# 64 instead of 32 tokens of the second layer gather the rows of their own experts, and 44 instead of 40 blocks of activations stay on chip

## The chip, the cores and the metric

The kernel runs on one core of a Trainium2 chip. The metric is device time in microseconds of one execution. Before the change it is 2793.98 us, the median of three runs (2786.86 to 2801.69). TensorE multiplies 128x128 matrices held as weights with up to 512 columns, VectorE and ScalarE work on tiles of 128 partitions, GpSimd (POOL) issues the gathers, SyncE (SP) and ScalarE issue the other transfers; all transfers run on the core's 16 DMA engines.

## The reference

Two layers over 512 tokens (256 of context, 256 latent, 1024 features). Each layer has four parallel mixers (neighbourhood attention, an mLSTM, latent attention, window attention) and then an expert stage, which is what matters here:

```python
def peer_ffn(h, wq, sub_keys, u, v):
    ...
        eidx = jnp.take_along_axis(cand_i, fpos, axis=-1)
        gate = jax.nn.softmax(fs, axis=-1)
        act = jax.nn.gelu(jnp.einsum('td,thkd->thk', xb, u[eidx]).astype(F32), approximate=False)
        w = (gate * act).astype(xb.dtype)
        return jnp.einsum('thk,thkd->td', w, v[eidx])
```

Each token chooses 128 of 16384 experts (8 heads, 16 each). For every chosen expert it takes the dot product with that expert's row of u (1024 floats), a gelu, a gate, and adds the row of v with that weight. In the second layer only the 256 latent tokens go through it.

## The kernel before, in words

Two ways of doing the expert stage stand side by side. Most tokens are done densely: all 16384 rows of u, as 128 blocks of 128 experts, are multiplied with all tokens (the U blocks), and all rows of v likewise (the V blocks); the gates are a matrix that is zero where a token did not choose an expert. A few tokens, the ones "apart", are done by gathering: GpSimd fetches the rows of u and v that these tokens chose, and VectorE makes the dot products and sums.

`APART` holds their number for each layer (128 and 32). With fewer than 128 such tokens each has 128/n partitions, each partition serving n of its 128 experts; in the second layer that is four partitions of 32 before. One gather (line 1409) fetches one row of 4 KB for each of 128 partitions, 0.524 MB; there are n of them for u, each followed by a multiplication with a sum on VectorE (line 1415, tile `junk`), and n for v, each followed by a multiply-add (lines 1420 and 1422, tile `facc`). At the end `facc` is added over a token's partitions with a matmul (line 1548, `fsel`). `wd` is the number of tokens left for the dense way: 224 in the second layer.

A U block: SP loads two blocks at once (line 1446, tile `raw`, two buffers of 1 MB), ScalarE rounds a block to the short format of TensorE (line 1448, tile `spl`, ten buffers), VectorE takes the remainder (line 1449), TensorE makes 24 matmuls with `wd` columns (three products, lines 72 to 74, for each of 8 slices), ScalarE the gelu (line 1466). The activations of the first 2 x `FOLD` blocks stay on chip (`kept`), the others are stored (`ad`) and loaded again for V.

Gates: for every 8 tokens VectorE builds three kinds of one-hot tiles (lines 1351, 1352, 1354), TensorE multiplies them (line 1368, 16 matmuls), ScalarE copies the part of the blocks that are not kept (line 1371, `gstage`), which is stored for every 32 tokens (line 1377, `gd`), and VectorE multiplies the kept activations in place (line 1375).

A V block: SP loads rows of v (line 1489), the gates of four blocks (line 1494, `vg`) and the activations of two (line 1497, `va`); VectorE multiplies gates and activations (line 1503, for blocks that were not kept), ScalarE and VectorE split weights (1504, 1505) and rows (1508, 1509) in two parts, and TensorE makes for each of 8 slices one matmul with both parts of the weights side by side (line 1519, 2 x `wd` columns) and one with `wd` columns (line 1521).

The program is written as loops of Python generators: `u_next` (line 1143 on) interleaves U blocks with gathers so that `PHASE1` steps of gathering are done by the last U block, and `rows_to` spreads the remaining ones over the first 58 pairs of V. In U, gathered rows take turns with the blocks in the ten `spl` buffers; in V they have four buffers of their own (`ROWS`). A scheduler that runs when the program is built then sets the order on each engine; the engines run that order without changing it. SP's transfers too are issued in that order, so one that has to wait holds up those behind it.

Of the kernel before, what the change touches and what calls it, by code (L numbers as in the profile page):

```python
# [29 lines left out]
PIECE = 3  # L30
F_ML, F_NA, F_MLA, F_SW = (1.3, 2.0), (1.0, 1.2), (1.2, 1.2), (1.2, 1.0)
RN, GW, GL = (2, 1), 1.4, (3, 3)
FOLD, QS, VA = (0, 20), (10, 6), (2, 3)

CTX = slice(0, TC)
LAT = slice(TC, TA)
APART = (128, 32)
ROWS = 4
PHASE1 = (144, 26)

C_ID = 0
C_RS = 128
# [11 lines left out]
class Kernel:  # L54
# [39 lines left out]
    def build(self):  # L94
        tc, nc, A = self.tc, self.nc, self.A
        with ExitStack() as es:
# [24 lines left out]
            self.ms = cst.tile([128, 4], F32, name="ms")  # L121
            self.wd = [TA - APART[0], TC - APART[1]]
            self.gd = [self.dram.tile([self.wd[l] // 32, 128, 128, 32], F32, name=f"gd{l}") for l in range(L)]
# [919 lines left out]
    def peer(self, l):  # L1043
# [4 lines left out]
        wd = self.wd[l]  # L1048
        apart = APART[l]
        t0 = apart // 128  # L1050
        with ExitStack() as es:
# [14 lines left out]
            def u_pair():  # L1066
                i = next(ublk, None)
                if i is not None:
                    used[0] += 1
                    self.u_blocks(l, i, dh, dl, wd)  # L1070
            with ExitStack() as e1:
# [45 lines left out]
                with ExitStack() as e2:  # L1117
# [20 lines left out]
                    def rows_to(n):  # L1138
                        while sp is not None and s0[0] < n:
                            s0[0] += 1  # L1140
                            next(sp, None)

                    def u_next():
                        u_pair()
                        rows_to(PHASE1[l] * (used[0] - u0) // (64 - u0))
                    for n, _ in enumerate(routes[t0]):
# [32 lines left out]
                with ExitStack() as e2:  # L1179
# [16 lines left out]
                    for n, i in enumerate(self.v_order(l)):  # L1196
                        rows_to(PHASE1[l] + (2 * apart - PHASE1[l]) * n // 58 if n < 58 else 300)
                        self.v_blocks(l, n, i, acc, ts, w - wd)
# [158 lines left out]
    def gates(self, l, t, g, hot):  # L1357
# [6 lines left out]
        for q in range(2):  # L1364
# [7 lines left out]
            if nf:  # L1372
                o = t * 128 + g * 8 + 4 * q - APART[l]
                f = self.kept[:, :, o:o + 4]
                nc.vector.scalar_tensor_tensor(f, pg[:, :nf], 1.0 / GSCALE, f, op0=ALU.mult, op1=ALU.mult)
        if g % 4 == 3:
            nc.scalar.dma_start(self.gd[l][4 * t + g // 4 - APART[l] // 32][:, nf:], self.gst)

# [439 lines left out]
```

## Time and profile before

| | before |
|---|---|
| median of the runs | 2793.98 us |
| the profiled execution, its own time | 2801.05 us |
| its span, first to last instruction | 2799.3 us |
| TensorE busy | 2628.3 us (94%) |
| VectorE busy | 2168.7 us (77%) |
| ScalarE busy | 1249.8 us (45%) |
| GpSimd busy | 490.9 us (18%) |
| DMA | 691.48 MB, mean 247 GB/s |

The shares are means over the whole program. The second layer's expert stage lies in the last 810 us of the span: its queries until about 2080, the U blocks until about 2425, the V blocks after that. A busy TensorE is not one at its peak, since matmuls overlap: how fast it goes is seen from the starts of successive matmuls. A DMA share can go over 1, since it adds up the durations of packets, which overlap.

### The profile page before, as it was taken

The page shows a single profiled execution, that of the slowest core. Times are in us where ns is not written, and L with a number is a line of the kernel's source. Part 1 is how long each engine was busy: PE and PEld are TensorE (multiplying, and loading weights), DVE is VectorE, ACT ScalarE, POOL GpSimd, SP SyncE. Part 2 cuts the span into 40 slices and gives each one's busy share as a digit, 9 for nine tenths or more (in the row PEclk, how much of TensorE's full clock was granted, in tenths as well). Part 3 has the DMA queues.
Part 4 walks back from the last instruction along what each step waited for, and adds up shares of the span by engine and source line. Part 5 has one row for each costly group of instructions (what it writes and reads, how often), then busy time and mean ns, then how long its engine had stood idle before and what let it go on. Part 6 is the DMA issues. An engine that isn't in the chain of part 4 may idle for free. (4 is left out here: it accounts for less than half of the span.)

```text
span 2799.3 us, 44568 instructions
## 1 busy us (share of the span) xinstructions
PE 2628.3 (94%) x17143; PEld 2407.9 (86%) x17143; DVE 2168.7 (77%) x4499; ACT 1249.8 (45%) x2059; POOL 490.9 (18%) x419
## 2 busy tenths in 40 slices
PE   8989899999999999799999998988999999998998
PEld 5766768999998898799999997767899999898987
DVE  5665757999998886699999886565788777677776
ACT  4564645334344433343333334554545444444443
POOL 0010000003443234233333320000001111111110
PEclk9999899999999999899999999999999999999999
DMA  7110424647998989989999993211535787998984
GB/s 264 69 61 31 166 89 157 220 159 246 347 359 337 340 321 378 338 322 386 382 367 384 372 364 125 76 39 68 201 137 191 270 283 282 333 319 294 333 306 167
DMA packets 275733, 691.48 MB, mean 247 GB/s; under 512 B 18016, under 2 KB 145376, under 8 KB 266048
## 3 DMA queue, kind: packets, MB, share of 16 engines
q1 hardware_dynamic: 196608, 448.12, 45.6%
q0 software_dynamic: 46080, 167.79, 15.9%
q10 hardware_dynamic: 32832, 72.72, 6.9%
q8 instruction: 134, 2.20, 0.3%
q14 instruction: 79, 0.65, 0.1%
HBM read 616.56 MB, written 71.57 MB: 246 GB/s over the span
## 5 line engine op out<-in xcount | busy, mean ns | idle before, releaser
L72 PE MATMUL pu<-h2h,spl 128*128 128x384 f32 (+1 forms) x2048 | 637.8, 311 | 37.1 <-ACT spl L1448 28.0
L74 PE MATMUL pu<-h2h,spl 128*128 128x384 f32 (+1 forms) x2048 | 629.6, 308 | 2.9 <-DVE spl L1449 2.9
L73 PE MATMUL pu<-h2l,spl 128*128 128x384 f32 (+1 forms) x2048 | 630.2, 308 | 0.0
L72 PEld LDWEIGHTS pu<-h2h,spl 128*128 128x128 f32 x2048 | 394.2, 192 | 44.9 <-ACT spl L1448 32.7
L74 PEld LDWEIGHTS pu<-h2h,spl 128*128 128x128 f32 x2048 | 393.5, 192 | 4.8 <-DVE spl L1449 4.6
L73 PEld LDWEIGHTS pu<-h2l,spl 128*128 128x128 f32 x2048 | 394.2, 192 | 0.3
L1509 DVE TENSOR_TENSOR spl<-raw,spl 128x1024 fp32r<-128x1024 f32 x256 | 305.7, 1220 | 98.2 <-ACT spl L1508 92.5
L1448 ACT CAST spl<-raw 128x1024 fp32r<-128x1024 f32 x256 | 266.3, 1051 | 249.2 <-DMA raw<-in_ut 92.3
L1508 ACT CAST spl<-raw 128x1024 fp32r<-128x1024 f32 x256 | 261.9, 1051 | 256.5 <-DMA raw<-in_v 173.6
L1449 DVE TENSOR_TENSOR spl<-raw,spl 128x1024 fp32r<-128x1024 f32 x256 | 311.7, 1224 | 44.1 <-ACT spl L1448 32.6
L73 PE MATMUL f<-wt,spl 128*128 128x384 f32 x1024 | 343.2, 335 | 0.0
L74 PE MATMUL f<-wt,spl 128*128 128x384 f32 x1024 | 336.3, 334 | 0.0
L72 PE MATMUL f<-wt,spl 128*128 128x384 f32 x1024 | 288.4, 337 | 2.1 <-ACT spl L1508 1.9
L1519 PE MATMUL f<-wt,spl 128*128 128x448 f32 x1024 | 251.1, 372 | 17.1 <-ACT spl L1508 11.7
L1409 POOL DMA_INDIRECT spl<-in_un,ix x97 | 131.6, 1357 | 704.8 <-DVE fp L1263 241.6
L1466 ACT ACTIVATE act<-pu 128x384 f32<-128x384 f32 (+1 forms) x216 | 93.7, 436 | 299.3 <-PE pu L74 268.8
L1519 PEld LDWEIGHTS f<-wt,spl 128*128 128x128 f32 x1024 | 186.0, 190 | 33.3 <-ACT spl L1508 15.0
L427 DVE TENSOR_TENSOR spl<-raw,spl 128x512 fp32r<-128x512 f32 (+1 forms) x226 | 149.8, 702 | 64.0 <-ACT spl L423 55.0
L73 PEld LDWEIGHTS f<-wt,spl 128*128 128x128 f32 x1024 | 193.0, 188 | 0.5 <-issue 0.5
L74 PEld LDWEIGHTS f<-wt,spl 128*128 128x128 f32 x1024 | 191.6, 188 | 0.0
L72 PEld LDWEIGHTS f<-wt,spl 128*128 128x128 f32 x1024 | 187.9, 189 | 3.2 <-ACT spl L1508 2.2
L1409 POOL DMA_INDIRECT row<-in_vn,ix x87 | 125.7, 1445 | 369.6 <-DVE facc L1422 313.0
(326 smaller groups left out, 5029.2 us busy)
## 6 DMA issues: line engine op xcount, KB each, us to landing
raw<-in_ut SPq DMA_DIRECT2D x128, 1024.0 KB
raw<-in_v SPq DMA_DIRECT2D x128, 1024.0 KB
ad<-act ACTq DMA_DIRECT2D x64, 384.0 KB
gd<-gstage ACTq DMA_DIRECT2D x12, 2048.0 KB
vg<-gd SPq DMA_DIRECT2D x32, 768.0 KB
va<-ad SPq DMA_DIRECT2D x64, 384.0 KB
raw<-in_win SPq DMA_DIRECT2D x22, 1024.0 KB
raw<-in_wq SPq DMA_DIRECT2D x16, 1024.0 KB
```

Of the source, the lines that this page charges most:

```text
L72: mm(ps, ah, bh, start=first, stop=False, **kw)
L73: mm(ps, ah, bl, start=False, stop=False, **kw)
L74: mm(ps, al, bh, start=False, stop=last, **kw)
L427: return eng.tensor_tensor(p[1][o], w[:, o], p[0][o].bitcast(F32), op=ALU.subtract)
L1409: nc.gpsimd.indirect_dma_start(r, None, tabs[which], bass.IndirectOffsetOnAxis(ix[:, s:s + 1], 0))
L1448: self.pin(nc.scalar.copy(uh, self.u[:, n % 2]), n < 3)
L1449: self.pin(nc.vector.tensor_tensor(ul, self.u[:, n % 2], uh.bitcast(F32), op=ALU.subtract), n < 3)
L1466: nc.scalar.activation(a[:, b, :w], ps[:, :w], AF.Gelu)
L1508: nc.scalar.copy(vh, v[:, b])
L1509: nc.vector.tensor_tensor(vl, v[:, b], vh.bitcast(F32), op=ALU.subtract)
L1519: nc.tensor.matmul(acc[d][:, off:off + 2 * w], vh[:, c], both, start=first, stop=last)
```

## The change

Three numbers change for the second layer. 64 tokens are apart, each on two partitions, so that 64 gathers of u and 64 of v are made and the dense way has 192 tokens (24 groups of gates for 28). 44 blocks of activations are kept for 40. 60 steps of gathering are placed by the last U block, for 26.

```diff
-FOLD, QS, VA = (0, 20), (10, 6), (2, 3)
+FOLD, QS, VA = (0, 22), (10, 6), (2, 3)
...
-APART = (128, 32)
+APART = (128, 64)
 ROWS = 4
-PHASE1 = (144, 26)
+PHASE1 = (144, 60)
```

The scheduler makes another order of this. On VectorE, this is how the last gates stand towards the U blocks. Before (`spl<-raw` is the split of a U block at line 1449 and of a V block at 1509, `kept` the gates at 1375):

```order
L1375 SCALAR_TENSOR_TENSOR kept<-pg,kept 128x40x4
L1449 TENSOR_TENSOR spl<-raw,spl 128x1024
L1422 SCALAR_TENSOR_TENSOR facc<-spl,wt,facc 128x1024
L1449 TENSOR_TENSOR spl<-raw,spl 128x1024 x2
L1375 SCALAR_TENSOR_TENSOR kept<-pg,kept 128x40x4
L1449 TENSOR_TENSOR spl<-raw,spl 128x1024
L1505 TENSOR_TENSOR wt<-kept,wt 128x2x224
L1509 TENSOR_TENSOR spl<-raw,spl 128x1024 x3
```

And now:

```order
L1375 SCALAR_TENSOR_TENSOR kept<-pg,kept 128x44x4
L1449 TENSOR_TENSOR spl<-raw,spl 128x1024
L1422 SCALAR_TENSOR_TENSOR facc<-spl,wt,facc 128x1024
L1449 TENSOR_TENSOR spl<-raw,spl 128x1024
L1505 TENSOR_TENSOR wt<-kept,wt 128x2x192 x2
L1415 SCALAR_TENSOR_TENSOR junk,dots<-spl,ht 128x1024
L1449 TENSOR_TENSOR spl<-raw,spl 128x1024
L1422 SCALAR_TENSOR_TENSOR facc<-spl,wt,facc 128x1024
L1449 TENSOR_TENSOR spl<-raw,spl 128x1024 x3
L1503 TENSOR_TENSOR va<-va,vg 128x384 x2
```

Before, one split of a U block stands behind the last gates; now twenty do (six of them shown), with gathered rows between them and the first weights of V (`wt`, `va`) among them.

On SP, the loads from the tokens' indices (`own`) to the first rows of v (`in_v`). Before:

```order
L1388 DMA own<-fin_18884 32x3x32 x4
L1446 DMA raw<-in_ut 128x2x1024 x42
L1489 DMA raw<-in_v 128x2x1024 x2
L1494 DMA vg<-gd_85 128x7x128
L1497 DMA va<-ad_87 128x2x224 x2
```

And now:

```order
L1388 DMA own<-fin_18884 64x3x64 x2
L1446 DMA raw<-in_ut 128x2x1024 x35
L1494 DMA vg<-gd_85 128x6x128
L1497 DMA va<-ad_87 128x2x192 x2
L1494 DMA vg<-gd_85 128x6x128
L1497 DMA va<-ad_87 128x2x192
L1446 DMA raw<-in_ut 128x2x1024 x2
L1494 DMA vg<-gd_85 128x6x128
L1497 DMA va<-ad_87 128x2x192
L1446 DMA raw<-in_ut 128x2x1024 x2
L1494 DMA vg<-gd_85 128x6x128
L1446 DMA raw<-in_ut 128x2x1024 x3
```

The last seven loads of U now stand behind loads of gates (`vg`) and activations (`va`), of which the first reads what the last gate store wrote. Gates and activations are loaded in the same order as before otherwise, 21 and 42 times instead of 22 and 44.

## Rows read from the trace of the kernel before

**Rows 1.** Cores: span, mean granted clock of TensorE.

```profile
core 0: 2799.3 us, clock 0.973
```

**Rows 2.** Stretches: length, busy (count) of PE, PEld, DVE, ACT, POOL; clock; DMA share; GB/s.

```profile
800.00:1000.00 200.00, 184.47 (x1323) 174.84 (x1322) 179.03 (x246) 85.12 (x136) 68.26 (x49) 0.97 0.91 341
1200.00:1600.00 400.00, 400.00 (x2309) 400.00 (x2308) 365.37 (x462) 140.51 (x149) 143.42 (x93) 1.00 1.03 375
1988.00:2130.00 142.00, 139.92 (x1227) 139.55 (x1227) 124.41 (x505) 77.95 (x127) 0.00 (x0) 1.00 0.50 173
2145.00:2425.00 280.00, 267.00 (x2540) 265.05 (x2540) 214.21 (x307) 135.69 (x234) 45.02 (x30) 0.98 0.79 279
2425.00:2785.00 360.00, 337.34 (x2092) 315.11 (x2092) 259.90 (x308) 161.96 (x199) 38.42 (x34) 0.99 0.85 296
```

**Rows 3.** Timeline of TensorE in U: start, duration, line, tiles, shape, count.

```profile
2329.77 0.27 PE L73 MATMUL pu<-h2l,spl 128*128 128x224 f32 x1
...
2333.23 0.27 PE L74 MATMUL pu<-h2h,spl 128*128 128x224 f32 x1
2333.35 0.64 PE L1368 MATMUL pg<-at,bt 128*128 128x128 f16 x8
```

**Rows 4.** Groups of TensorE, 2145 to 2425: busy us, mean ns, idle before.

```profile
L1368 PE MATMUL pg<-at,bt 128*128 128x128 f16 x448 | 32.7, 221 | 7.7 <-DVE kept L1375 7.7
```

**Rows 5.** Timeline of TensorE in V.

```profile
2629.75 1.79 PE L1519 MATMUL f<-wt,spl 128*128 128x448 f32 x8
2631.38 1.05 PE L1521 MATMUL f<-wt,spl 128*128 128x224 f32 x8
2632.27 1.79 PE L1519 MATMUL f<-wt,spl 128*128 128x448 f32 x8
```

**Rows 6.** Waits, 2430 to 2780: us in total, times, longest.

```profile
ACT spl L1508 <- DMA raw<-in_v: 131.1, 57, 5.1
```

**Rows 7.** Timeline of TensorE in the first layer: 256 columns, then 2 columns.

```profile
299.80 0.28 PE L267 MATMUL fp<-spl,cs 128*128 128x256 f32 x1
...
300.28 0.28 PE L267 MATMUL fp<-spl,cs 128*128 128x256 f32 x1
...
300.71 0.60 PE L285 MATMUL mm<-cmb,adarow 4*128 4x2 f32 x4
```

**Rows 8.** Line 285: duration in ns, least/median/most; first and last start.

```profile
L285 PE MATMUL mm<-cmb,adarow x48: 246/246/366, 288.2 to 336.6; 4*128 4x2 f32 x48
```

**Rows 9.** Groups of VectorE, 2145 to 2425.

```profile
L1449 DVE TENSOR_TENSOR spl<-raw,spl 128x1024 fp32r<-128x1024 f32 x85 | 103.2, 1222 | 17.7 <-ACT spl L1448 10.8 <-PE pu L73 3.5 <-PE pu L74 2.9
L1354 DVE TENSOR_TENSOR at<-eq,parts 128x1024 f16<-128x1024 f16 x56 | 36.3, 687 | 0.0
L1415 DVE SCALAR_TENSOR_TENSOR junk<-spl,ht 128x1024 f32<-128x1024 f32 x16 | 19.6, 1223 | 17.0 <-DMA spl<-in_un,ix 17.0
...
L1375 DVE SCALAR_TENSOR_TENSOR kept<-pg,kept 128x160 f32<-128x160 f32 x56 | 16.6, 320 | 15.4 <-ACT gstage L1371 15.3
L1422 DVE SCALAR_TENSOR_TENSOR facc<-spl,wt,facc 128x1024 f32<-128x1024 f32 x7 | 9.0, 1282 | 6.3 <-DMA spl<-in_vn,ix 6.3
```

**Rows 10.** DMA queues, 2145 to 2425: packets, MB, share of 16 engines.

```profile
q1 hardware_dynamic: 11654, 44.98, 46.1%
q10 hardware_dynamic: 12432, 19.73, 19.1%
q0 software_dynamic: 3588, 13.09, 13.7%
```

**Rows 11.** DMA queues and issues (KB each), 2425 to 2785.

```profile
q1 hardware_dynamic: 48938, 85.31, 69.1%
q0 software_dynamic: 5628, 20.47, 14.8%
...
raw<-in_v SPq DMA_DIRECT2D x62, 1024.0 KB
```

**Rows 12.** Groups of VectorE, 2425 to 2785.

```profile
L1505 DVE TENSOR_TENSOR wt<-va,wt 128x448 fp32r<-128x448 f32 x44 | 27.2, 621 | 9.0 <-ACT wt L1504 9.0
```

## The prediction

> **What bounds the kernel now.** I read the busy time by stretch first, since the change touches only the second layer's expert stage. The profiled execution has a span of 2799.3 us [rows 1] inside a time of 2801.05 us; the median of the runs is 2793.98, so I make the sum against the profiled execution and set its difference on the median, 7 us lower. Two stretches hold nearly all that changes [rows 2]: the U stretch, 2145 to 2425 (280 us), where blocks of the first table are multiplied while gates are built and the first rows are gathered, and the V stretch, 2425 to 2785 (360 us). The reader is to see that TensorE is busy nearly throughout both while the DMA engines are at 0.79 and 0.85 and VectorE at 214 and 260 us: three resources close together, none with much room.
>
> How full TensorE really is comes from the spacing of its matmuls, not from their length (they overlap). In the U stretch 32 of 224 columns start within 3.46 us [rows 3], the first and the last of them shown: 0.112 apart. The stretch has 2540 matmuls [rows 2], 448 of them the gates' (28 groups of 16; eight in 0.64 us, where one lasts 0.22, are 0.06 apart [rows 3, 4]), so 87 blocks of 24: 87 x 24 x 0.112 + 448 x 0.06 = 261 us, 0.931 of 280. In the V stretch eight matmuls of 448 columns take 1.63 us and eight of 224 take 0.89 [rows 5]: 0.204 and 0.111. 64 pairs of blocks with 16 of each are 323 us, 0.935 of the 345 us until the last accumulation (about 2770). So TensorE is the fullest in both, but the waits already name other things: in V ScalarE waits 131 us for V's rows to land [rows 6].
>
> **The change part by part.**
>
> *Narrower matmuls.* 192 columns replace 224, and 384 replace 448. With 256 columns the spacing is 0.12 (five starts in 0.48 us) [rows 7]; with 384 it is 0.173, the first layer's V stretch, 2309 matmuls in 400 us without a gap [rows 2]. That is 0.053 per 128 columns, by which 224 would be 0.107 and 192 would be 0.093. But 224 is at 0.112, above that line, and four matmuls of 2 columns behind their own weight loads still need 0.60 us [rows 7], which is 0.12 each when one lasts 0.25 [rows 8]. I read that as a floor of about 0.11, the weight load. Then 192 columns cost what 224 cost: nothing is won in U, nor in V's short matmuls, and V's long ones win 1024 x (0.204 - 0.173) = 32 us. Bounds: 0 and 19 ns for each short one; I take 0. The Trainium skill, "TensorE: Matmul & The Clock Gate", section "LDWEIGHTS (loading the stationary operand)", gives a load's time as its columns over 1.2, about 107 ns for 128: near the 0.112 here. The same page's isolated spacing ("Back-to-back issue gap", N/2.4 + 2.5 ns) would make 224 columns 96 ns and 192 columns 82, and the trace has 112 for the first; its sum is with the rivals.
>
> *Fewer tokens in the gates.* 24 groups of 8 tokens, not 28. Each costs VectorE four passes of 0.687 and two of 0.32 [rows 9]: 4 x 3.39 = 13.6 us less; the two become 10% wider, +1.5 us. TensorE loses 64 x 0.06 = 4 us.
>
> *Twice the gathers.* 128 gathers of 0.524 MB, not 64. By the order of VectorE, 56 of their multiplications stand before the last U block where 24 stood, and 72 behind it where 40 stood: +32 in each stretch, half at 1.223 and half at 1.282 [rows 9]: +40 us of VectorE in each. For the DMA engines: in U, 13.7% of 280 us for 13.09 MB (25 gathers) is 1.53 us each, +49 us; in V, 14.8% of 360 for 20.47 MB (39) is 1.37, +44 us [rows 10, 11].
>
> *Less of activations and gates through memory.* Six gate stores of 1.38 MB for seven of 1.44, 42 activation stores of 0.197 MB for 44 of 0.229 (44 blocks kept, not 40): 3.5 MB less, at 19.1% of 280 us for 19.73 MB (2.7 us per MB) 9.5 us less in U [rows 10]. Read back in V: 16.5 MB for 20.2. V's own rows, 62 x 1.05 = 65 MB, at U's 2.87 us per MB (46.1% of 280 for 44.98) take 187 of the queue's 249 us, so the other 20.3 MB take 62, 3.1 per MB: 3.7 MB are 11 us [rows 10, 11]. The multiplication and the split of V's weights go from 448 columns and 0.62 us [rows 12] to 384, which I put at 0.55 (in proportion 0.53), with two multiplications fewer: about 9 us of VectorE off.
>
> *What moves.* SP's order now has four loads of gates and four of activations ahead of the last seven loads of U. The first waits for the last gate store, and these U loads are queued behind it. On ScalarE 20 casts of U blocks stand behind that store, 14 of them the seven loads' own, so 6 blocks of 24 x 0.112 = 2.69 us, 16 us, cover a store that lasts some 4 us (1.38 MB at 2.7). I cost the wait at nothing; without cover it is those 4 us. It moves 2.4 MB, 7 us of DMA, from V into U, and 7 of V's weight passes (4 us of VectorE).
>
> *Sum for U.* VectorE 214 + 40 - 14 + 2 + 4 = 246 us; DMA 221 + 49 - 9.5 + 7 = 268; TensorE 257. These are uneven: the gates now end 20 blocks before U does. Up to there VectorE has 66 splits of 1.222, 24 groups of 3.45 and 43 gathers, 81 + 83 + 53 = 217 us, against TensorE's 66 x 2.69 + 23 = 200; behind it TensorE leads with 54. The bound is 217 + 54 = 271. At the fullness that the leading engine has today, 0.931, that is 291 us, and the DMA engines' 268 would give 288. So VectorE takes TensorE's place: +11 us. From both sides: 271 without any wait (-9), and VectorE's 246 with all of today's idle 66 us kept, 312 (+32). The first layer's stretch 800 to 1000 has TensorE at 0.92, VectorE at 0.90 and DMA at 0.91 together [rows 2], so such a mixture runs near 0.92; I stay with +11.
>
> *Sum for V.* TensorE 323 - 32 = 291; VectorE 260 + 40 - 9 - 4 = 287; DMA 306 + 44 - 11 - 7 = 332, now the fullest. At 0.935 that is 354 us for today's 345: +9. Bounds: the whole relief of TensorE (-32), and DMA no fuller than now (306/345 = 0.887), 373 us (+28).
>
> Costed at nothing: fewer copies of the tokens' vectors and indices (two for four, one for three, once, under the matmuls of 1988 to 2145), 64 columns for 32 in the 16 closing matmuls (under the floor), narrower activations on ScalarE, which is busy under half of both stretches.
>
> Together +20: 2801 + 20 = 2821 in the profiled execution's terms, and 2794 + 20 = **2814** against the median.
>
> **Rivals.**
> *V's transfers simply get denser (the other side).* In the first layer's V stretch, 1200 to 1600, DMA is at 1.03 with TensorE without a gap [rows 2]. If the second layer reaches that, V needs 332/1.03 = 322 us, with VectorE's 287 at that row's 0.91 (315) and TensorE's 291 at 0.935 (311) inside it: -23, and with U at +11 the kernel takes 2782, not slower. It decides from a share of 332/334 = 0.99 on. Against it: a pair of blocks there has 48 matmuls of 0.173 (8.3 us) for V's two buffers to refill, here 345/64 = 5.4, and ScalarE waits for that refill now [rows 6].
> *192 columns are quicker than 224.* At 0.093 the 41 blocks ahead of the U stretch, where TensorE is busy 139.9 of 142 us [rows 2], gain 41 x 24 x 0.019 = 19 us, and the 20 blocks behind the gates come down from 54 to VectorE's 45 us (-9); the rest stays with VectorE and DMA. +20 - 28 = -8: 2786. For it: 224 is only 5 ns above the line; against it the 2-column matmuls. By the Trainium skill's isolated spacing (page and section above) the step from 224 to 192 is 13 ns, and the first gain would be 13 us.
> *In-order waits add up.* VectorE already waits 17.0 us for gathered rows in U at 16 dots [rows 9]. If its idle time stays whole while its work grows, and V's transfers get no denser, both upper bounds hold: +32 + 28 = +60, 2854. Against it: part of that idle time is there because TensorE was behind.
>
> **How the numbers follow.** Forecast 53%, with its own range from 2794 to 2836: the leading engine 0.03 fuller or emptier than now in each stretch (U 282 to 301, V 343 to 366). Denser transfers 22%, quicker short matmuls 8%, adding waits 17%. A measurement of this kernel tells about 0.5% (14 us) from no change: below 2780 faster, above 2808 slower. Faster: half of the second case and near half of the third: 0.16. Same: 30% of the forecast and most of what is left of these two: 0.30. Slower: 0.54. The range, 2780 to 2846, leaves out the low half of the dense case and the worst of the waits.
>
> **What would show it.** Short matmuls still 0.11 apart and long ones 0.173; VectorE near 246 and 287 us and DMA over 0.9 in both stretches; TensorE with more idle time than now in both; the U stretch about 11 us longer with the gates ending well before it. The forecast is wrong if the 192-column spacing falls under 0.10, if V gets shorter, or if U stays at 280 us.

## The result, and the profile after

The changed kernel takes 2824.36 us (median of 4 runs, 2809.51 to 2829.18), beside 2791.32 us for the kernel before on the same chip (4 runs): ratio 1.0112 [1.0079, 1.0144]. On another chip it was 2827.49 beside 2796.12, ratio 1.0106 [1.0063, 1.0149]. So it is slower by 1.1%, some 31 to 33 us, where 20 were forecast; 2824 lies inside the range.

The profiled execution is the quickest of the four, 2809.51 us, 8.5 above that of before. Its span:

```profile
core 0: 2807.7 us, clock 0.969
```

The two stretches are cut here by events, not by round numbers: U begins when the tokens' indices are ready and ends with its last matmul, and V ends with the first closing matmul. The columns are those of [rows 2]. First before, then after:

```profile
2141.00:2428.00 287.00, 273.55 (x2597) 271.42 (x2596) 218.57 (x314) 137.69 (x237) 45.02 (x30) 0.98 0.79 280
2428.00:2776.00 348.00, 327.37 (x2023) 306.07 (x2024) 252.80 (x291) 159.06 (x193) 38.42 (x34) 0.99 0.87 303
```

```profile
2130.00:2432.00 302.00, 280.29 (x2537) 275.69 (x2535) 247.99 (x349) 133.13 (x235) 90.73 (x64) 0.95 0.89 323
2432.00:2787.00 355.00, 310.52 (x2030) 303.24 (x2028) 280.63 (x332) 155.78 (x192) 73.83 (x64) 0.97 0.91 322
```

U is 15 us longer and V 7. That is 22 in the stage, while the execution is only 8.5 longer: U starts 11 us earlier, after work that the change hardly touches (the first U blocks, which stand there, have 192 columns now), and the first layer's stretch 800 to 1000 ran at a clock of 0.99 here and 0.97 there [rows 2]. So this execution is a lucky one ahead of the stage. The second chip's profile (below, "again") shows 34 in the stage, and that is what the medians say.

U in two parts, up to the last gate and behind it, says where the time sits:

```profile
2130.00:2357.00 227.00, 215.09 (x2017) 211.84 (x2015) 201.52 (x297) 103.56 (x188) 69.21 (x45) 0.97 0.86 310
2357.00:2432.00 75.00, 65.20 (x523) 63.86 (x521) 46.47 (x53) 29.57 (x47) 21.51 (x19) 0.91 0.99 364
```

Behind the gates, the last blocks of U (523 matmuls, some 22 blocks of 24) take 75 us. TensorE is busy for 65, VectorE for 46, and the DMA engines for 0.99 of it. What they carry there (queues: packets, MB, share of the 16 engines; issues: KB each, median us to landing):

```profile
q0 software_dynamic: 2876, 10.47, 36.1%
...
raw<-in_ut SPq DMA_DIRECT2D x9, 1024.0 KB, 9.3
...
vg<-gd SPq DMA_DIRECT2D x4, 384.0 KB, 8.7
va<-ad SPq DMA_DIRECT2D x4, 192.0 KB, 13.8
```

A third of the engines' time there is gathers (q0), and a U load takes 9.3 us to land.

TensorE's own spacing is close to the forecast (0.11 and 0.173). In U, 30 starts in 3.24 us, the first and the last shown, are 0.112 apart at 192 columns; in V (next fence) eight of 384 columns take 1.43 us, 0.179 each, and eight of 192 take 0.87:

```profile
2399.82 0.27 PE L74 MATMUL pu<-h2h,spl 128*128 128x192 f32 x1
...
2403.06 0.28 PE L73 MATMUL pu<-h2l,spl 128*128 128x192 f32 x1
```

```profile
2603.32 1.03 PE L1521 MATMUL f<-wt,spl 128*128 128x192 f32 x8
2604.19 1.59 PE L1519 MATMUL f<-wt,spl 128*128 128x384 f32 x8
2605.62 0.58 PE L1521 MATMUL f<-wt,spl 128*128 128x192 f32 x4
```

The waits in V (us in total, times, longest):

```profile
ACT spl L1508 <- DMA raw<-in_v: 108.1, 49, 4.5
...
PE f L1519 <- ACT spl L1508: 41.2, 25, 3.9
```

The second of these rows in the kernel before, 2430 to 2780:

```profile
PE f L1519 <- ACT spl L1508: 11.7, 14, 1.6
```

ScalarE waits for V's rows less than before, 108 us for the 131 of [rows 6]. But TensorE now waits for ScalarE's split for 41 us, where before it had 11.7 us. The wait has not grown; it has come through to TensorE, whose work is shorter.

The granted clock is lower too. TensorE in V in pieces of 10 us (the columns of [rows 2]):

```profile
2440.00:2450.00 10.00, 8.14 (x54) 7.80 (x53) 7.89 (x11) 4.82 (x6) 2.70 (x2) 0.99 0.89 317
2450.00:2460.00 10.00, 10.00 (x62) 10.00 (x61) 7.78 (x10) 4.87 (x6) 1.92 (x2) 0.84 0.79 248
...
2470.00:2480.00 10.00, 7.02 (x47) 6.86 (x48) 7.23 (x10) 4.43 (x6) 1.02 (x1) 1.00 1.02 378
2480.00:2490.00 10.00, 7.79 (x55) 7.62 (x54) 7.79 (x11) 4.40 (x7) 2.81 (x3) 1.00 0.91 311
2490.00:2500.00 10.00, 10.00 (x61) 10.00 (x60) 8.60 (x10) 3.26 (x4) 2.82 (x2) 0.83 0.97 338
...
2650.00:2660.00 10.00, 10.00 (x73) 10.00 (x72) 7.56 (x9) 3.32 (x5) 0.16 (x1) 1.00 0.86 294
```

Read the second and the fifth line against the last: TensorE is busy for the whole 10 us in all three, yet does 62 and 61 matmuls there and 73 at the full clock. A mean of 0.84 is a third of the time at the lower level, 1.2 GHz, and two thirds at 2.4. Both slow pieces follow one in which TensorE stood idle for about 2 us of 10. But idle time alone does not decide it: the fourth line follows a piece with 3 us of it and ran at 1.00. Over the stretches the clock fell from 0.98 to 0.95 in U and from 0.99 to 0.97 in V. 0.03 of 302 us and 0.02 of 355 are 9 and 7 us of work at the full clock (an estimate from these rows).

### The profile page after: what moved, and what is told of

Its sections match the earlier page's. It is cut to its first block, busy times and chain, and to the rows that moved or that the text cites. A ratio compares the mean times of both kernels' runs of the same rounds, so it can differ in the third digit from the quotient of the medians.

```text
span 2807.7 us, 44651 instructions
## 1 busy us (share of the span) xinstructions
PE 2612.7 (93%) x17079; PEld 2404.9 (86%) x17079; DVE 2224.6 (79%) x4571; ACT 1237.7 (44%) x2055; POOL 562.1 (20%) x483
## 4 chain that ended last, share of the span: by engine, by line
PE 36%; DVE 8%; DMA 8%; issue 6%; ACT 2%; POOL 1%; SPq 1%; ACTq 0%; POOLq 0%; DVEq 0%
PE f L72 6%; PE f L73 6%; PE f L74 6%; DMA raw<-in_ut 4%; DVE spl L1449 2%; PE pu L72 2%; PE pu L74 2%; PE pu L73 2%; DMA raw<-in_v 2%; PE f L1519 2%; PE fp L72 1%; PE fp L73 1%; POOL row L1409 1%; PE fp L74 1%; PE f L1521 1%
## 5 line engine op out<-in xcount | busy, mean ns | idle before, releaser
L73 PE MATMUL f<-wt,spl 128*128 128x384 f32 x1024 | 343.1, 335 | 0.0
L74 PE MATMUL f<-wt,spl 128*128 128x384 f32 x1024 | 336.3, 334 | 0.0
L72 PE MATMUL f<-wt,spl 128*128 128x384 f32 x1024 | 288.5, 337 | 2.1 <-ACT spl L1508 1.9
L1409 POOL DMA_INDIRECT spl<-in_un,ix x114 | 153.3, 1345 | 660.8 <-DVE fp L1263 241.5
L1519 PE MATMUL f<-wt,spl 128*128 128x384 f32 x1024 | 219.2, 351 | 41.6 <-ACT spl L1508 41.2
L1409 POOL DMA_INDIRECT row<-in_vn,ix x102 | 143.4, 1406 | 332.4 <-DVE facc L1422 280.9
```

What stands on the lines that cost most here:

```text
L72: mm(ps, ah, bh, start=first, stop=False, **kw)
L73: mm(ps, ah, bl, start=False, stop=False, **kw)
L74: mm(ps, al, bh, start=False, stop=last, **kw)
L1409: nc.gpsimd.indirect_dma_start(r, None, tabs[which], bass.IndirectOffsetOnAxis(ix[:, s:s + 1], 0))
L1519: nc.tensor.matmul(acc[d][:, off:off + 2 * w], vh[:, c], both, start=first, stop=last)
```

## The experiments

The theory at the start was the prediction's: VectorE holds back the first part of U, and the transfers hold back V. Its rival was that the transfers alone are the price, in both stretches. U and V are cut by events throughout.

**again: the changed kernel once more, on the chip of the next three.** No edit.

> The changed kernel unaltered, beside the kernel before on the same chip, to see how much of the measured 33 us lies in the second layer's expert stage. Theory (VectorE is the fullest engine in U, the DMA engines in V): U stretch (from the tokens' indices to the last U matmul) 296 to 304 us against 287 before, V (first V matmul to the closing matmuls) 352 to 358 against 347: +17 to +28 us; what the median shows beyond that lies ahead of this stage, where the programs are the same. Rival: the stage itself is 30 us longer in the usual execution and the first profile was a lucky one.

Measured: 2827.49 us (2815.57 to 2833.67). Its U and V:

```profile
2136.00:2441.00 305.00, 281.95 (x2548) 277.67 (x2547) 248.97 (x351) 135.11 (x238) 90.17 (x64) 0.96 0.89 321
2441.00:2805.00 364.00, 315.37 (x2025) 307.04 (x2026) 280.19 (x332) 155.18 (x192) 84.93 (x64) 0.95 0.89 313
```

U is 18 us longer than before and V 16: V varies between executions by more than I thought, with the clock (0.95 here, 0.97 above).

**half_dma: every second gather of the second layer left out.** The multiplication reads the row gathered last, so VectorE's work stays whole.

```diff
         def gather(which, s):
+            if l and s % 2:
+                return self.last[which]
             r = self.row_tile()
+            self.last[which] = r
...
+        self.last = {}
```

> The changed kernel with half of the second layer's gathers left out: every second multiplication takes the row of the one before it again, so VectorE has all 128 multiplications and the DMA engines 64 gathers; the output is not the reference's. Theory (VectorE bounds U, DMA bounds V): U stays near 296 (VectorE 243 us as now, DMA down by about 49), V falls to 318 to 328 (DMA 288, VectorE 287, TensorE 291 us of work): 25 to 35 us faster than the changed kernel, about 2792. Rival (the transfers alone are the price in both stretches): U falls to about 284 and V to 318, about 2775. Rival (VectorE alone is the price): V stays at 355, U at 300: 2820.

Measured: 2777.59 us, ratio to before 0.995 [0.9924, 0.9975], 50 us under "again".

```profile
2133.00:2419.00 286.00, 271.81 (x2540) 268.70 (x2540) 247.94 (x348) 132.05 (x237) 49.54 (x34) 0.99 0.79 281
2419.00:2749.00 330.00, 303.36 (x2026) 293.50 (x2024) 277.77 (x334) 154.69 (x192) 41.16 (x30) 0.99 0.86 298
```

VectorE is as busy as in the changed kernel (248 and 278 us), and U is back at 286: the theory, by which U had to stay near 296, falls. V at 330 shows what the narrower matmuls are worth once the gathers are back at the old number: 348 to 330.

**half_mul: all gathers, every second multiplication left out.** The counterpart.

```diff
...
             r = gather(0, s)
+            if l and s % 2:
+                return
...
             r = gather(1, s)
+            if l and s % 2:
+                return
```

> The changed kernel with all 128 gathers of the second layer but only every second multiplication on VectorE; the output is not the reference's. Theory: U falls to about 287 (VectorE 206 us, TensorE 257, DMA 268, which now is the fullest), V stays at 350 to 356, where DMA is the fullest: 10 to 16 us faster than the changed kernel, about 2812. Rival (transfers alone): U and V stay: 2824. Rival (VectorE alone): U 278, V 320: about 2768.

Measured: 2831.18 us, ratio 1.0127 [1.0093, 1.0161], no quicker than the changed kernel.

```profile
2145.00:2452.00 307.00, 282.27 (x2530) 277.87 (x2528) 214.87 (x302) 133.25 (x233) 86.41 (x66) 0.94 0.88 320
2452.00:2808.00 356.00, 307.17 (x2027) 296.56 (x2025) 239.50 (x282) 154.37 (x193) 74.81 (x62) 0.99 0.89 318
```

VectorE is 33 and 41 us less busy, below the kernel before, and neither stretch gains. So VectorE's multiplications are not what this change pays for, in U or in V.

**half_both: gathers and multiplications both halved.** The same two lines, ahead of the gather.

```diff
         def dot(s):
+            if l and s % 2:
+                return
             r = gather(0, s)
...
```

> The changed kernel with every second gather of the second layer and its multiplication left out: the dense way has 192 tokens as in the changed kernel, the gathers are as many as before the change; the output is not the reference's. It prices the narrower dense way by itself. Theory: U about 276 (TensorE 257 us), V about 315 (TensorE 291): 50 to 65 us faster than the changed kernel, about 2765, and 20 to 35 faster than the kernel before. Rival (the new order, gates that end early and gate loads ahead of U's, or the clock, is what costs): it stays within 10 us of 2815.

Measured: 2796.45 us, ratio 0.9993 [0.9971, 1.0015]. That is 31 us under "again", but 19 us over half_dma, which does more.

```profile
2136.00:2434.00 298.00, 277.54 (x2537) 275.09 (x2537) 215.91 (x301) 131.45 (x235) 53.83 (x32) 0.96 0.74 263
2434.00:2776.00 342.00, 305.99 (x2032) 299.01 (x2031) 237.88 (x283) 155.86 (x193) 35.97 (x33) 0.98 0.84 292
```

In its U, VectorE waits for gathered rows at the dot products for 28.9 us, in half_dma for 4.2. Half_both, half_dma and, for comparison, phase28 (below):

```profile
DVE junk L1419 <- DMA spl<-in_un,ix: 28.9, 10, 4.5
DVE junk L1419 <- DMA spl<-in_un,ix: 4.2, 4, 1.7
DVE junk L1415 <- DMA spl<-in_un,ix: 24.7, 12, 5.8
```

VectorE comes to the dots earlier and then stands in order before a row that has not landed, which would fit the rival of adding waits. But phase28 has nearly as much of this wait in U, as many bytes to move there (78 MB) and as much work on VectorE and TensorE, and its U takes 278 us. So this wait does not explain the 19 us; they stay open.

**narrow_u: the kernel before, with 23 of each U block's 24 matmuls in the second layer at 192 columns.** The columns beyond 192 get one product only.

```diff
-                self.mm3(ps[:, :w], uh[:, k], ul[:, k], hh[k], hl[k], k == 0, k == KD - 1)
+                if l:
+                    mm, n = nc.tensor.matmul, 192
+                    mm(ps[:, :w] if k == 0 else ps[:, :n], ...
+                    mm(ps[:, :n], uh[:, k], hl[k][:, :n], start=False, stop=False)
+                    mm(ps[:, :n], ul[:, k], hh[k][:, :n], start=False, stop=(k == KD - 1))
...
```

> The kernel before, with 23 of the 24 matmuls of each U block of the second layer cut from 224 to 192 columns and nothing else changed (the last 32 tokens' dot products are left incomplete, so the output is not the reference's). Theory (a floor of about 0.11 us set by the weight load): the spacing stays at 0.111 to 0.112, the queries' stretch stays at 145 us, U at 283 to 291, the time at 2790 to 2802. Rival (the columns count, 0.093): the queries' stretch shrinks by about 18 us, U by 10 to 35, the time to 2740 to 2770.

Measured: 2791.04 us beside 2791.19, ratio 1.0002 [0.9985, 1.0019]. Its U:

```profile
2131.00:2418.00 287.00, 273.89 (x2591) 272.16 (x2590) 218.57 (x314) 137.27 (x236) 44.02 (x30) 0.98 0.78 276
```

287 us and 273.9 busy, as before with 224: narrowing the short matmuls wins nothing.

**phase44 and phase28: fewer of the gathers ahead of the end of U.** Of 128 steps of gathering, 60 are placed by the last U block in the changed kernel; here 44 and 28. The name says how many.

```diff
-PHASE1 = (144, 60)
+PHASE1 = (144, 44)
```

> The changed kernel with 44 steps of gathering placed by the last U block, not 60: 16 gathers, 22 to 24 us of transfers, move from U to V; nothing is left out. Theory as the first four runs leave it (the DMA engines are the price in both stretches): U loses 6 to 12 us (292 to 298), V gains 8 to 18 (365 to 375), the time stays within 8 us of the changed kernel's 2827. Rival (the stall is in U, from gates that end early and gate loads standing ahead of U's rows): U comes back to 287 to 290 with V unchanged, about 2812. Rival (VectorE): U loses 16 us, V gains little: 2813.

> The changed kernel with 28 steps of gathering by the last U block: nearly the number that U had before the change, so that all additional gathers are in V; nothing is left out. Theory (DMA): U 284 to 290 as before the change, V 380 to 395 (its DMA work grows by 44 us on top of the 326): 2832 to 2848. Rival (V has room, as the first layer's V stretch at a DMA share of 1.03 suggests): V 360 to 365, 2805 to 2815.

Measured: 2826.65 us, ratio 1.013 [1.0082, 1.0178], and 2831.01 us, ratio 1.0142 [1.0111, 1.0173]. Their U and V, phase44 first:

```profile
2133.00:2432.00 299.00, 277.66 (x2542) 274.39 (x2541) 229.24 (x321) 130.81 (x234) 66.04 (x48) 0.97 0.83 291
2432.00:2808.00 376.00, 317.21 (x2026) 308.65 (x2027) 299.48 (x359) 155.65 (x194) 106.21 (x80) 0.95 0.93 332
```

```profile
2136.00:2414.00 278.00, 269.70 (x2544) 267.85 (x2544) 212.80 (x299) 132.87 (x234) 46.41 (x31) 0.99 0.79 281
2414.00:2807.00 393.00, 325.12 (x2027) 315.35 (x2026) 318.40 (x383) 155.49 (x196) 130.28 (x98) 0.93 0.94 341
```

In phase28 U falls to 278 us and V rises to 393: 671 together (675 in phase44) where the changed kernel takes 657 and, in "again", 669. The gathers cost the same wherever they stand. Phase44 also has the loads of gates back behind the last loads of U, and gains nothing by it.

With the gathers, the place of the gates changes too. In the changed kernel, "again", half_mul and fold20 the last gates stand 75 to 83 us before the end of U, in raw3 (below) 91. In half_dma, half_both, no_gather and half_bytes the scheduler has them back at 13 to 17 us, so these runs change two things in U at once. Phase44 and phase28 show what the late gates are worth when all gathers are made: their last gates start 22 and 16 us before the end (duration in ns, least/median/most; first and last start):

```profile
L1375 DVE SCALAR_TENSOR_TENSOR kept<-pg,kept x48: 327/333/341, 2154.3 to 2410.1; 128x176 f32<-128x176 f32 x48
L1375 DVE SCALAR_TENSOR_TENSOR kept<-pg,kept x48: 328/333/342, 2156.8 to 2397.6; 128x176 f32<-128x176 f32 x48
```

U and V together are no shorter for it. That speaks against the later gates as the gain of the runs with fewer gathers. It is no proof, since these two runs also move gathers into V.

**fold20: the changed kernel with 40 blocks kept, as before.**

```diff
-FOLD, QS, VA = (0, 22), (10, 6), (2, 3)
+FOLD, QS, VA = (0, 20), (10, 6), (2, 3)
```

> The changed kernel with 40 blocks of activations kept, as before the change: two more pairs are stored and loaded again (0.8 MB) and one more load of gates (0.4 MB); nothing is left out. Theory (DMA): 3 to 5 us of transfers more, the time 2825 to 2834, not to be told from the changed kernel. Rival (keeping more blocks costs, by the wider multiplication on VectorE and the order that the scheduler makes of it): 5 to 15 us faster than the changed kernel.

Measured: 2828.96 us, ratio 1.0137 [1.0114, 1.0159], with U at 308 and V at 362. The interval overlaps that of the changed kernel, so this part of the change cannot be told from nothing.

**no_gather: no gathers and no multiplications in the second layer.**

```diff
...
         def dot(s):
+            if l:
+                return
...
```

> The changed kernel with all gathers of the second layer and their multiplications left out (the 64 tokens' part is zero, so the output is not the reference's). It shows what the dense way with 192 tokens needs alone. Theory (transfers, through the gaps that they leave in TensorE, are the price of the gathers): U 268 to 278 us (TensorE's work is 257), V 305 to 315 (291): U and V together 575 to 590 against 656 to 668 in the changed kernel, the time 2725 to 2750. Rival (something else in the changed stage, its order or the split of weights and rows on ScalarE and VectorE, sets the pace): U and V together stay above 615.

Measured: 2732.88 us, ratio 0.9778 [0.9751, 0.9805].

```profile
2139.00:2405.00 266.00, 266.00 (x2535) 265.00 (x2533) 184.97 (x262) 131.83 (x231) 0.00 (x0) 1.00 0.69 240
2405.00:2705.00 300.00, 293.38 (x2025) 289.30 (x2024) 197.35 (x228) 149.83 (x187) 0.00 (x0) 1.00 0.79 269
```

This is TensorE by itself: no gap in U, the clock at 1.00 throughout. Beside it the changed kernel's U has 14 us more busy time for the same matmuls and 22 us of gaps. All the gathers with their multiplications cost about 94 us against "again", 0.74 us for each of 128, where the prediction had put 1.37 to 1.53 us of DMA time on each: about half of a gather's transfer comes through.

**half_bytes: 128 gathers of half a row.** Each brings 512 numbers, not 1024, and the multiplications have that width.

```diff
             r = self.row_tile()
+            if l:
+                nc.gpsimd.indirect_dma_start(r[:, :512], None, tabs[which], ...
+                return r[:, :512]
...
```

> The changed kernel with all 128 gathers of the second layer, each of which takes 512 of a row's 1024 numbers, and multiplications of that width; the output is not the reference's. Bytes as with 64 gathers, transfers as many as with 128. Theory (bytes): U and V together 615 to 645 us, as in the two runs with 64 gathers, 2775 to 2800. Rival (the number: GpSimd's issue, a buffer held for each, a wait for each landing): 655 to 670, about 2822.

Measured: 2778.54 us, ratio 0.9947 [0.9923, 0.997].

```profile
2138.00:2427.00 289.00, 273.50 (x2537) 270.51 (x2535) 217.30 (x345) 131.50 (x234) 78.36 (x62) 0.98 0.80 275
2427.00:2755.00 328.00, 304.64 (x2022) 299.94 (x2021) 243.52 (x335) 154.89 (x192) 75.92 (x66) 0.97 0.86 302
```

That is half_dma's time with twice its number of gathers: between these two the price is by bytes, not by transfers. Bytes alone do not fix the time, though: half_both gathers as many of them and takes 18 us more.

**raw3 and before_raw3: a third buffer for the 1 MB loads, in the changed kernel and in the kernel before.** For the memory, the split buffers go from ten to eight. Both numbers hold for both layers.

```diff
-RAW, SPL, WQS = 2, 10, (6, 5)
+RAW, SPL, WQS = 3, 8, (6, 5)
```

> The changed kernel with three buffers of 1 MB for the rows of u and v, not two, paid for with eight split buffers, not ten, in both layers; nothing is left out. Theory (U's and V's rows land too late behind the gathers, and two buffers can't cover it; the bytes themselves still fit): U and V together fall by 15 to 35 us to 630 to 650. Rival (the DMA engines' throughput is the bound): 655 to 670, unchanged. Rival (split buffers matter more): above 675.

> The kernel before with three buffers for the rows of u and v and eight split buffers, in both layers; nothing is left out: the control for the run above. Theory (late landings): U and V together 620 to 634 against 634 to 636, as TensorE's 582 us of work leave less to win than in the changed kernel; the time 2770 to 2795. Rival (split buffers matter more): above 645.

Measured: raw3 2813.6 us, ratio 1.0051 [1.0026, 1.0076]; before_raw3 2807.61, ratio 1.0044 [1.0028, 1.006]. Their U and V, raw3 first:

```profile
2169.00:2479.00 310.00, 284.57 (x2558) 282.14 (x2558) 249.36 (x350) 133.53 (x237) 96.73 (x64) 0.94 0.88 319
2479.00:2799.00 320.00, 296.98 (x2025) 291.40 (x2024) 280.77 (x335) 156.05 (x193) 94.18 (x64) 0.99 0.96 353
```

```profile
2171.00:2447.00 276.00, 269.57 (x2571) 267.65 (x2571) 215.02 (x311) 133.94 (x234) 41.78 (x30) 0.99 0.81 291
2447.00:2777.00 330.00, 320.87 (x2031) 305.25 (x2029) 255.58 (x292) 158.29 (x194) 52.41 (x34) 0.99 0.91 316
```

And raw3's waits in V:

```profile
ACT spl L1508 <- DMA raw<-in_v: 15.3, 18, 3.3
```

V falls to 320 us with every gather in it, the DMA share rises from 0.91 to 0.96, and ScalarE's wait for V's rows goes from 108 to 15 us. So in V the engines had room; the two buffers did not let the loads use it. U gains nothing (310). But both kernels reach U about 30 us later (raw3 33 to 39), so raw3 keeps only 14 us against the changed kernel, and before_raw3 loses 11 against the one before. One place where it goes is the first layer's V stretch, where TensorE had no gap [rows 2] and now has:

```profile
1200.00:1600.00 400.00, 385.59 (x2197) 381.63 (x2196) 346.58 (x435) 134.17 (x141) 130.20 (x87) 1.00 0.99 353
```

I put that on the eight split buffers. The eight and the three were not run apart, and a third buffer in the second layer's stage alone was not tried. No kernel that computes everything beat the one before.

The two runs also show how much of the change's price hangs on the two buffers. With a third one in both kernels the change costs 6 us by the medians (2813.6 for 2807.61), where it cost 31, and the two intervals overlap. The profiles show 24 us in the stage (630 for 606: U 34 longer, V 10 shorter), but raw3's is the slowest of its five executions.

## Why the prediction was right, and where it was not

**The direction and the size: right.** Forecast +20 (U +11, V +9); measured 31 to 33 by the medians, and in the stage +15 and +7 in one execution, +18 and +16 in the other.

**Narrower matmuls: right.** The floor holds: 0.112 at 192 columns, and narrow_u moves nothing. By the Trainium skill, "TensorE: Matmul & The Clock Gate", section "LDWEIGHTS (loading the stationary operand)", a weight load takes its columns over 1.2 in ns, by estimate about 107 ns for 128. The trace agrees with its 0.112 between starts. The long matmuls gave less than the 32 us priced: TensorE's busy time in V fell by 17. About 7 of the missing 15 are the lower clock, by the estimate above. In no_gather, at a clock of 1.00, it fell by 34 (327 to 293), so the price was about right for TensorE undisturbed.

**Work of the engines: right.** VectorE 248 and 281 us (246 and 287 forecast), DMA 0.89 x 302 = 269 and 0.91 x 355 = 323 (268 and 332).

**SP's order: nothing seen against putting it at nothing.** The prediction named 4 us if the loads behind the last gate store had no cover. SP waits for that store for 2.4 us here:

```profile
SPq L1494 <- DMA gd<-gstage: 2.4, 1, 2.4
```

Phase44 has the old order, and its two stretches together are no shorter.

**"VectorE takes TensorE's place" in U: wrong.** This is the step that failed, though its sum came near. Half_mul takes 33 us of VectorE's work out of U and U does not get shorter. Of the two parts of the bound, the first (217 us at 0.931, 233) was measured at 227, for another reason than VectorE's work. The second, behind the gates, was put at TensorE's 54 (58 at that fullness) and measured at 75 with the DMA share at 0.99; that it held 22 blocks, not 20, explains 5 of it. I had added up U's 268 us of transfers over the whole stretch and found them just below the bound. They are not spread evenly: the gates end 75 us before U does (in the kernel before, 12 us), TensorE then asks for a new block every 2.69 us instead of sharing the time with gates, and nearly a third of the gathers (19 of 64) and the moved loads of gates and activations fall into those 75 us. A sum of transfers for each part, as I had made one for VectorE, would have shown this tail. Whether it would have given the price is not shown: without the tail, but with gathers moved into V, phase44 and phase28 are no quicker. What the runs do show is that U's price comes with the gathers' transfers (no_gather's U is 266 us) and not with VectorE's work.

**V: right in size, half right in cause.** The forecast was DMA as the fullest resource at 0.935 of 354 us (332/0.935 is 355); it was 0.91 of 355. But 0.91 is no limit of the engines: with a third buffer, 0.96. What limits V, by raw3 and its control (320 for 355, 330 for 348), is that a 1 MB load of two blocks can be asked for only when one of two buffers is free, while gathers share the way it comes by. The first rival (V's transfers get denser) had priced that at 322 us, and raw3's V takes 320. The objection made against it, that a pair of blocks gives the two buffers too little time to refill, was the right one.

**The term that was missing: TensorE's clock fell.** The prediction scaled the bound by today's fullness, and so took the matmuls' length as given. In U, TensorE's busy time rose by 7 us though 64 gate matmuls (4 us) were gone, at a clock of 0.95 for 0.98. The low clock goes with gaps in most of these stretches (none, and 1.00, in no_gather's U), but not in all: half_mul's V has 49 us of gaps at 0.99. No run set the clock apart from the gaps, so its share remains an estimate.

**In-order waits: wrong for the changed kernel.** VectorE's idle time ahead of the dots is below the 17.0 us of [rows 9] in spite of twice as many of them (us busy, mean ns; idle before, and its cause):

```profile
L1415 DVE SCALAR_TENSOR_TENSOR junk<-spl,ht 128x1024 f32<-128x1024 f32 x32 | 38.9, 1217 | 11.4 <-DMA spl<-in_un,ix 11.4
```

**Open:** why the first part of U takes 227 us when neither VectorE's work (half_mul: 229) nor the third buffer (raw3: no faster) decides it, although no_gather shows that the gathers do; and half_both's 19 us over half_dma, with U at 298 where phase28 needs 278 for the same bytes and work in another order.

## What to carry to other kernels

Sum the transfers for each part of a stretch between two changes of pace, not for the stretch: an average of 0.89 held a tail of 75 us at 0.99. That says where time sits; whether it is the price, only a run without it says (phase44 was no quicker). When work is taken off the fullest engine and given to transfers, ask how many loads can be in flight before asking how many bytes go through: two buffers of 1 MB gave V 0.91 of the DMA engines, three gave 0.96 and 35 to 44 us. And halve each suspect by itself: VectorE was nearly as full as TensorE, and halving its multiplications won nothing.

## What the runs showed of the hardware that was not expected

A short wait of TensorE can cost twice, and need not. Two pieces of 10 us that follow one with 2 us of idle time ran at a mean granted clock of 0.83 or 0.84 and did 61 or 62 matmuls instead of 73. A piece that follows one with 3 us of idle time ran at 1.00, and half_mul's V kept 0.99 with 49 us of gaps. Without gathers, where U has no gap, the clock stayed at 1.00.

A gather of half a row cost about half in this pair of runs: 128 gathers of 512 numbers and 64 of 1024 ended within 1 us of each other (2778.54 and 2777.59, on two chips whose kernel before differs by 0.1 us).
